# A two-layer decoder trunk on one core: VectorE takes over GpSimd's work at three entries, and the first loads are reordered

## The chip, the cores and the metric

One core of a Trainium2 chip runs the whole program. The metric is the device time of one execution in microseconds (us). The kernel before took 1767.41 us in the median of three runs (1766.88 to 1770.72). TensorE (PE) does the matrix products, ScalarE (ACT) and VectorE (DVE) the elementwise work, GpSimd (POOL) a little of it too; SyncE (SP) issues nearly all loads.

## The reference

256 tokens of 1024 channels go through two layers. A condition vector gives shift, scale and gate per channel (adaLN). Each layer has a mixer (convolution branch and chunkwise retention with rotary angles, one common input projection `w_in`) and a channel part: a dense SwiGLU in layer 0, eight experts with the top two per token in layer 1. After each part stands a post-norm residual.

```python
c_act = jax.nn.silu(c)
for l in range(DEPTH):
    ada = c_act @ w_ada[l] + b_ada[l]
    shift1, scale1, gate1, shift2, scale2, gate2 = ...
    h = x * (1.0 + scale1) + shift1
    mix = token_mixer(h, positions, w_in[l], ...)
    x = layer_norm(DEEPNORM_ALPHA * x + gate1 * mix, ln1_g[l], ln1_b[l])
    h = x * (1.0 + scale2) + shift2
    ff = swiglu(h, ...) if l % 2 == 0 else moe_swiglu(h, ...)
    x = layer_norm(DEEPNORM_ALPHA * x + gate2 * ff, ln2_g[l], ln2_b[l])
```

## The kernel before

**Precision and units.** Every product is done in three: a weight block `wf` (1 MB, 128x2048) is split into a high half `wh` (a cast on ACT, line 1678) and a low half `wl` (a subtraction on DVE, line 1680), 1024 columns at a time, and so are the activations (hH and hL, rH and rL, mH and mL, aH and aL, hgH and hgL). PE then adds wh·hi, wh·lo and wl·hi. A unit of the program is one such block with the function that uses it; `prog` is the list of units and of pieces of code between them, and the last loop of `_emit` walks it, splits some pieces ahead (`look`, `split_to`, at most six halves in buffers), runs what was deferred (`defer(k, f)`: k splits later), and issues a load as soon as a buffer was consumed. Each engine works through its own list in that order; only semaphores tie them.

**Start (lines 215 to 250, 658 to 712).** For k from 0 to 7 a column block `adat` (summed against the condition on DVE, line 260, into `adac`) is followed by an S block of `w_in`. `first_h` makes h of 128 channels on POOL: fh, hH, hL (lines 674 to 677). `products` then adds the block's 48 matmuls into eight banks (line 661). `rope_tables` makes the sine and cosine of the positions (lines 1069 to 1087). The loads on SP stand in the order: condition, columns, positions, column block 0, two blocks of xT, S block 0, the rest of xT.

**Entries of the dense layer and of layer 1's mixer.** `out_units` ends the part before: tile 0 (128 tokens) is normalized (`z_norm`), tile 1 after it. `boundary` gives what comes next: units of the gate (`fill`), `tile_to_h` for each tile (transposes, then hf_t with the new shift and scale, then hHn on ACT and hLn on POOL, line 388), and `close_ln`, which updates x with the norm's own g and b on POOL (lines 405 and 406, four steps of 128x1024), then closes the buffers. `T_unit` (dense) or `V_unit(0, ...)` (mixer) does the first products of tile 0 before tile 1 is ready. The buffers of the next stage (`sg`, `v`) lie where g and b lay.

**Entry of the experts (`moe`).** `ahead(4, pool)` has POOL split the first four low halves. Each tile is transposed (`turn`), routed (`logits`, `top`, `rank`, `onehot`), turned back (`back`) and split (`split_h`: hTH, hTL); x is updated on POOL; four `gather` steps make the experts' rows (hgH on ACT, hgL on DVE). The first two expert blocks are loaded into the buffers that hgH and hgL take later. `whole_h` adds hT on POOL. After that the experts' units follow, six matmuls of 512 columns for each split piece.

Of the kernel before, what the change touches and what calls it, by code (L numbers as in the profile page):

```python
# [12 lines left out]
F32 = mybir.dt.float32  # L13
# [4 lines left out]
ALU = mybir.AluOpType  # L18
PSUM = bass.MemoryType.PSUM

P = 128
# [23 lines left out]
OPEN = (11, 19, 27)  # L45
HFL = 999
XS = 10
AZL = 238
AHF = -0.5
VS = 0  # L50
# [10 lines left out]
CL = (5, 2)  # L61
CD = (2, 3)
BK = (4, 4)
EARLY = (2, 2, 0)
BEF = (0, -1)
LOOK = (4, 4)
COJ = 0
# [46 lines left out]
def _emit(tc, ctx, a):  # L114
# [47 lines left out]
    def code(fn):  # L162
        prog.append(fn)
# [49 lines left out]
    def setup():  # L213
        row, one = mixc["cst"][0:1, 0:D], sel[0:1, :]
        cb = state["cb"] = state["hp0"].tile([P, D], F32, name="cb", tag="on")
        sp.dma_start(row, a["c"])
        pool.memset(one, 1.0)
        for q in range(2):
            ps = tp_bank()
            mm(ps, one, row[:, q * 512:(q + 1) * 512], True, True)  # L220
            act.activation(cb[:, q * 512:(q + 1) * 512], ps, AF.Silu)
        sp.dma_start(cols, a["cols"])
        sp.dma_start(mixc["pi"], a["pos"].partition_broadcast(P))
        st["go"] = True
        issue_dma(1)
        sp.dma_start(mixc["xT"][:, 0:2, :], a["xT"][:, 0:2, :])
        issue_dma(2)
        sp.dma_start(mixc["xT"][:, 2:8, :], a["xT"][:, 2:8, :])

        make_identity(nc, ident)  # L230
        dve.tensor_copy(adab.rearrange("p l n -> p (l n)"), col("b_ada", 0, L * 48))
        for n in (1, 4):
            v = adab[:, :, n * 8:n * 8 + 8]
            dve.tensor_scalar(v, v, 1.0, None, op0=ALU.add)
# [92 lines left out]
    def hold(on):  # L327
        if not on:
            st["hold"] = None
        elif st["hold"] is None:  # L330
            st["hold"] = st["cur"]
# [72 lines left out]
    def x_update(z, t):  # L404
        pool.tensor_tensor(x[:, t, :], z[:, t, :], state["g"], op=ALU.mult)
        pool.tensor_tensor(x[:, t, :], x[:, t, :], state["b"], op=ALU.add)

    def load_gb(p, l, which):
        g = p.tile([P, D], F32, name="gbuf")
# [29 lines left out]
    def mixer(l, raws, bound, fill=(), tail=()):  # L439
# [139 lines left out]
        def V_unit(h, half):  # L579
            def fn(s, w, wl):  # L580
                k0 = half * 4 + s * 2
                if k0 == 0:
                    R["V"] = [mm_bank(), mm_bank()]
                    R["held"] = []
                ts_block(R["V"][0], w, wl, state["hH"], state["hL"], k0, 2, tsl(0), k0 == 0, k0 == 6)
                state.pop("second_tile", nothing)()
                if h == 0 and l:
                    hold(True)
                    R["held"].append((w, wl, k0))
                    if k0 < 6:  # L590
                        return
                    hold(False)
                else:
                    R["held"] = [(w, wl, k0)]
                for (w_, wl_, k_) in R["held"]:
                    ts_block(R["V"][1], w_, wl_, state["hH"], state["hL"], k_, 2, tsl(1), k_ == 0, k_ == 6)
                run_bg(BG[l])
                if k0 == 6:
                    if h == 0 and l and VS:
                        split_to(st["cur"] + VS)  # L600
                    v = R["hp"].tile([P, 2, 512], F32, name="v")
                    for t in range(2):
                        act.copy(v[:, t, :], R["V"][t])
                    R["v", h] = v
            return named(f'V{l}', Unit(W["v"][h, half], 2048, fn))
# [60 lines left out]
        def first_h(k):  # L666
            def fn():
                if k == 0:
                    state["hH"] = keep.tile([P, 8, T], F32R, name="hH0", tag="hH")
                    state["hL"] = keep.tile([P, 8, T], F32R, name="hL0", tag="hL")  # L670
                v = adac[:, 0, 0:16].rearrange("p (n k) -> p n k", n=2)[:, :, k]
                dve.tensor_tensor(v, v, adab[:, 0, 0:16].rearrange("p (n k) -> p n k", n=2)[:, :, k], op=ALU.add)
                f = R["hp"].tile([P, T], F32, name="fh", tag="rot0", bufs=2)
                pool.tensor_scalar(f, mixc["xT"][:, k, :], adac[:, 0, 8 + k:9 + k], adac[:, 0, k:k + 1],
                                   op0=ALU.mult, op1=ALU.add)
                pool.tensor_copy(state["hH"][:, k, :], f)
                pool.tensor_tensor(state["hL"][:, k, :], f, state["hH"][:, k, :], op=ALU.subtract)
                have["h", k] = True
                products(k)
            return fn  # L680

        if l == 0:
            code(open_pool)
            code(lambda: state.update(hp0=R["hp"]))
            code(setup)
            for what, k in START:
                if what == "a":
                    u = ada_cols(0, 0, k, first_h(k))
                    u.look = 0
                    if k == 0:  # L690
                        code(lambda: rope_tables(R["hp"]))
                else:
                    u = S_unit(k)
                prog.append(u)
            code(lambda: R.update(y=keep.tile([P, 8, T], F32, name="ycv", tag="z")))
            code(setup_late)
        else:
            first, t0, second, t1, close = bound
            prog.extend(first)
            code(t0)  # L700
            prog.extend(second)
            code(lambda: state.update(second_tile=t1))
            prog.append(V_unit(0, 0))
            prog[-1].look = 2
            if BEF[1] >= 0:
                prog[-1].before = (first + second)[BEF[1]]
            code(close)
            code(open_pool)
            prog.append(V_unit(0, 1))
            units += [A_unit(i) for i in range(6)]  # L710
        for h in range(H):
# [227 lines left out]
    def boundary(ada, nfx):  # L939
        fill = gate_fill(ada, ("lnp", "fx", nfx))  # L940

        def tile_to_h(t):
            z, (gcol, bcol) = state["z"], state["mc"]
            if t == 0:
                state["hH"] = keep.tile([P, 8, T], F32R, name="hHn", tag="hH")
                state["hL"] = keep.tile([P, 8, T], F32R, name="hLn", tag="hL")
            h_from(state["lnp"], z[:, t, :], t, gcol, bcol, "AA" if t == 0 else "DD", (pool, pool))

        return fill[0:2], (lambda: tile_to_h(0)), fill[2:4], (lambda: tile_to_h(1)), close_ln

    def close_ln(update=True):
        flush_deferred()
        for t in range(2 * update):
            x_update(state["z"], t)
        state.pop("lns").close()
        state.pop("lnp")
        if state.get("ffn") is not None:
            state.pop("ffn").close()
# [13 lines left out]
    def ffn(raws, bound):  # L972
# [10 lines left out]
        def T_unit(half):  # L983
            def fn(s, w, wl):
# [8 lines left out]
                if k0 < 6:  # L993
                    return
                hold(False)
                for (w_, wl_, k_) in R["held"]:
                    ts_block(R["b"][1], w_, wl_, state["hH"], state["hL"], k_, 2, tsl(1), k_ == 0, k_ == 6)
                for t in range(2):
# [37 lines left out]
        prog[-1].look = 2  # L1036
        if BEF[0] >= 0:
            prog[-1].before = (first + second)[BEF[0]]
        code(close)
        code(open_pool)  # L1040
        prog.append(T_unit(1))
        units = [GU_unit(j) for j in range(2, KF)]
        rest = [r[0] for r in raws[len(raws) - NREST:]]
# [45 lines left out]
    def moe():  # L1089
# [132 lines left out]
                                      op0=ALU.is_equal)  # L1222
            R["oh", pair] = oh

        def whole_h():
            R["hT"] = keep.tile([P, 2, D], F32, name="hT", tag="z")
            pool.tensor_tensor(R["hT"], R["hTH"], R["hTL"], op=ALU.add)
            state["keep"] = keep

        def chunk(kp):  # L1230
            h = R["hT"][:, :, 2 * kp * P:(2 * kp + 2) * P]
# [240 lines left out]
        def ahead(n, eng=dve):  # L1472
            code(lambda: split_to(pos_of[units[0].idx, 0] + n - 1, eng))

        for u in fill:
            u.look = 0
        ahead(4, pool)
        code(lambda: turn(0, "AA"))
        prog.extend(fill[0:2])
        code(lambda: logits(0))  # L1480
# [2 lines left out]
        code(lambda: turn(1, "AD"))  # L1483
        code(lambda: back(0))
        code(lambda: split_h(0))
        code(lambda: logits(1))
        code(lambda: back(1))
        code(lambda: state.update(hfx=R["p"]))
# [2 lines left out]
        prog.append(fill[3])  # L1491
        code(lambda: onehot(0))
        code(lambda: split_h(1))
        for t in range(2):
            code(lambda t=t: x_update(state["z"], t))
        code(lambda: defer(XS, lambda: act.activation(x, x, AF.Copy, scale=ALPHA)))
        for kp in range(4):
            if kp == 0:
                code(open_hg)
            o = slice(2 * kp * P, (2 * kp + 2) * P)  # L1500
            code(lambda kp=kp, o=o: gather(0, kp, (R["hTH"][:, :, o], R["hTL"][:, :, o]), mm_bank))
            if 1 <= kp <= 2:
                ahead(4 + kp)
        code(whole_h)
        prog.append(units[0])
        code(lambda: close_ln(False))
        code(open_acts)
# [144 lines left out]
    def issue_dma(upto=None):  # L1652
        while st["dma"] < (len(units) if upto is None else upto):
# [6 lines left out]
            mine.append(u.idx)  # L1660
            live.append(p)
            u.wf = p.tile([P, 2048], F32, name="wf", tag=tag, bufs=bufs)
            sp.dma_start(u.wf[:, 0:u.n], u.src)
            u.w = {}
            u.issued = True
            st["dma"] += 1
# [144 lines left out]
```

## Time and profile before

| | |
|---|---|
| median of 3 runs | 1767.41 us |
| profiled execution | 1769.15 us, span 1767.4 us |
| PE busy | 1700.4 us (96%) |
| DVE busy | 1556.2 us (88%) |
| ACT busy | 1157.4 us (65%) |
| POOL busy | 144.0 us (8%) |
| mean granted clock of PE | 0.987 of full |

The profile is one execution; its times start with the span. A row of the timeline gives start, duration, engine, line, operation and tiles, and in brackets how long the engine was idle before it and what ended the wait. Busy time is no proof of a limit: an engine's busy span may hold a wait inside an instruction. PE's clock has two levels here, 1.00 and 0.50 of full.

### The profile page before, as it was taken

The numbers are of one execution on the slowest core, as the hardware profiler recorded it, in microseconds if no ns is written. First come the engines' busy times: TensorE is split into PE (matmuls) and PEld (weight loads), VectorE is DVE, ScalarE is ACT, GpSimd is POOL, SyncE is SP. The second block draws the span as 40 slices with busy tenths as digits, with TensorE's granted clock in tenths as the row PEclk, the third lists the DMA queues.
The fourth block names the chain that finished last, engine by engine and source line by source line (L and its number), as shares of the span: only waits on it lengthen the run. The fifth ranks groups of instructions, "written<-read, shape, count | busy, mean of one in ns | idle before, by whom it ended". The sixth has DMA issues, their size and how long they took to land. (4 is left out here: it accounts for less than half of the span.)

```text
span 1767.4 us, 23998 instructions
## 1 busy us (share of the span) xinstructions
PE 1700.4 (96%) x8896; PEld 1431.5 (81%) x8896; DVE 1556.2 (88%) x2126; ACT 1157.4 (65%) x1625; POOL 144.0 (8%) x102
## 2 busy tenths in 40 slices
PE   6999999999999999999997999999999999999996
PEld 5978877669998698888886888888888888887885
DVE  7799989876778679999878999999999999998996
ACT  3566787643444365567543878778787878787783
POOL 5300000022000300000005000200002000100001
PEclk9999999999999999999997999999999999999998
DMA  9644457866789454445575889899998999898891
GB/s 363 257 167 145 165 205 288 310 258 243 281 305 352 176 191 167 167 170 188 188 281 238 325 324 378 328 357 378 362 372 312 398 350 383 314 373 329 333 342 63
DMA packets 71102, 491.60 MB, mean 278 GB/s; under 512 B 7953, under 2 KB 8721, under 8 KB 13634
## 3 DMA queue, kind: packets, MB, share of 16 engines
q1 hardware_dynamic: 69122, 484.28, 73.1%
q0 software_dynamic: 1568, 5.45, 0.9%
q8 instruction: 72, 1.18, 0.3%
q14 instruction: 52, 0.43, 0.1%
q10 hardware_dynamic: 288, 0.26, 0.0%
HBM read 488.92 MB, written 1.05 MB: 277 GB/s over the span
## 5 line engine op out<-in xcount | busy, mean ns | idle before, releaser
L1680 DVE TENSOR_TENSOR wl<-wf,wh 128x1024 fp32r<-128x1024 f32 x815 | 991.9, 1247 | 87.1 <-ACT wh L1678 74.1
L1678 ACT CAST wh<-wf 128x1024 fp32r<-128x1024 f32 x819 | 840.7, 1051 | 170.7 <-PE ps_mm L137 104.2
L137 PE MATMUL ps_mm<-wh,hgH 128*128 128x512 f32 x704 | 282.6, 401 | 0.0
L137 PE MATMUL ps_mm<-wh,hgL 128*128 128x512 f32 x704 | 275.1, 391 | 0.0
L137 PE MATMUL ps_mm<-wl,hgH 128*128 128x512 f32 x704 | 274.5, 390 | 0.0
L468 ACT ACTIVATE tap<-upad,cols 128x256 f32<-128x256 f32 x300 | 130.1, 505 | 74.9 <-DVE ycv L480 74.6
L137 PE MATMUL ps_mm<-hHn,wh 128*128 128x256 f32 x576 | 164.6, 286 | 0.5 <-ACT wh L1678 0.5
L137 PE MATMUL ps_mm<-hHn,wl 128*128 128x256 f32 x576 | 163.7, 284 | 0.8 <-DVE wl L1680 0.8
L137 PE MATMUL ps_mm<-hLn,wh 128*128 128x256 f32 x576 | 163.7, 284 | 0.0
L137 PEld LDWEIGHTS ps_mm<-wh,hgL 128*128 128x128 f32 x704 | 132.1, 188 | 27.9
L137 PEld LDWEIGHTS ps_mm<-wl,hgH 128*128 128x128 f32 x704 | 132.5, 188 | 26.0 <-issue 1.0
L137 PEld LDWEIGHTS ps_mm<-wh,hgH 128*128 128x128 f32 x704 | 132.2, 188 | 25.8 <-issue 1.0
L137 PE MATMUL ps_mm<-wh,mb 128*128 128x512 f32 (+1 forms) x476 | 145.8, 380 | 0.0
L137 PEld LDWEIGHTS ps_mm<-hHn,wh 128*128 128x128 f32 x576 | 111.2, 193 | 1.2 <-ACT wh L1678 0.7
L137 PEld LDWEIGHTS ps_mm<-hHn,wl 128*128 128x128 f32 x576 | 111.3, 193 | 1.0 <-DVE wl L1680 1.0
L137 PEld LDWEIGHTS ps_mm<-hLn,wh 128*128 128x128 f32 x576 | 111.3, 193 | 0.4 <-issue 0.2
L137 PEld LDWEIGHTS ps_mm<-wh,mb 128*128 128x128 f32 x476 | 87.9, 188 | 17.5 <-issue 1.5
L480 DVE TENSOR_TENSOR ycv<-ycv,tap 128x1024 f32<-128x1024 f32 (+1 forms) x90 | 94.0, 1045 | 5.6 <-ACT tap L468 4.2
L137 PE MATMUL ps_mm<-wl,mb 128*128 128x512 f32 (+1 forms) x238 | 89.8, 377 | 0.0
L137 PE MATMUL ps_mm<-wh,hHn 128*128 128x512 f32 x208 | 84.5, 406 | 0.0
L137 PE MATMUL ps_mm<-wh,hLn 128*128 128x512 f32 x208 | 81.3, 391 | 1.7 <-POOL hLn L388 1.7
L137 PE MATMUL ps_mm<-wl,hHn 128*128 128x512 f32 x208 | 81.2, 390 | 0.1
(307 smaller groups left out, 2947.2 us busy)
## 6 DMA issues: line engine op xcount, KB each, us to landing
wf<-moe_gu SPq DMA_DIRECT2D x176, 1024.0 KB, 7.0
wf<-moe_d SPq DMA_DIRECT2D x75, 1024.0 KB, 6.5
wf<-adat SPq DMA_DIRECT2D x32, 1024.0 KB, 6.1
wf<-ws SPq DMA_DIRECT2D x24, 1024.0 KB, 5.1
wf<-ffn_gu SPq DMA_DIRECT2D x20, 1024.0 KB, 6.4
wf<-v SPq DMA_DIRECT2D x16, 1024.0 KB, 4.9
wf<-g SPq DMA_DIRECT2D x16, 1024.0 KB, 4.9
wf<-f SPq DMA_DIRECT2D x16, 1024.0 KB, 4.9
```

Source lines behind the costliest of these rows:

```text
L137: pe.matmul(out, lhsT, rhs, start=start, stop=stop)
L468: act.activation(t[:, c - c0, :], u[:, c, j:j + T], AF.Copy, scale=taps[:, c, j:j + 1])
L480: dve.tensor_tensor(y, y, prod[j][:, 0:n, :], op=ALU.add)
L1678: act.copy(w[:, 0:m], src)
L1680: eng.tensor_tensor(wl[:, 0:m], src, w[:, 0:m], op=ALU.subtract)
```

## The change

- Start: the first two units are loaded in two halves each; the positions come after S block 0, column block 1 before the rest of xT. The angle tables are made ahead of the second column block instead of the first (`ROPE`). h of block 0 is made by DVE (fh, hL) and ACT (hH) instead of POOL; blocks 1 to 7 stay on POOL.
- Dense layer and layer 1's mixer: hLn moves from POOL to DVE for both tiles; half of tile 1's hf_t moves from DVE to ACT (`"AD"`); x is updated by DVE, in four steps that are deferred by `XD`. The old buffers are closed, and the new ones opened, inside the unit (`turned`) instead of after it.
- Experts: the first four low halves are split by DVE, one of them in front of the end of tile 1's sums (`EARLY[2]`), one after the first `split_h`, two after the second. x is updated and hT added by DVE, most of it deferred past the first expert unit.

```diff
+ROPE = 1
+XD = (1, 2, 3, 3)
-EARLY = (2, 2, 0)
+EARLY = (2, 2, 1)
...
         sp.dma_start(cols, a["cols"])
-        sp.dma_start(mixc["pi"], a["pos"].partition_broadcast(P))
         st["go"] = True
         issue_dma(1)
         sp.dma_start(mixc["xT"][:, 0:2, :], a["xT"][:, 0:2, :])
         issue_dma(2)
+        sp.dma_start(mixc["pi"], a["pos"].partition_broadcast(P))
+        issue_dma(3)
         sp.dma_start(mixc["xT"][:, 2:8, :], a["xT"][:, 2:8, :])
...
+    def x_steps(z):
+        def step(t, first):
+            if first:
+                dve.tensor_tensor(x[:, t, :], z[:, t, :], state["g"], op=ALU.mult)
+            else:
+                dve.tensor_tensor(x[:, t, :], x[:, t, :], state["b"], op=ALU.add)
+        return [lambda t=t, first=first: step(t, first) for t in range(2) for first in (True, False)]
...
                     hold(False)
+                    state.pop("turned", nothing)()
...
+                if k == 0:
+                    dve.tensor_scalar(f, mixc["xT"][:, k, :], adac[:, 0, 8 + k:9 + k], adac[:, 0, k:k + 1],
+                                      op0=ALU.mult, op1=ALU.add)
+                    act.copy(state["hH"][:, k, :], f)
+                    dve.tensor_tensor(state["hL"][:, k, :], f, state["hH"][:, k, :], op=ALU.subtract)
+                    have["h", k] = True
+                    products(k)
+                    return
...
-                    if k == 0:
+                    if k == ROPE:
                         code(lambda: rope_tables(R["hp"]))
...
-            code(close)
-            code(open_pool)
+            code(lambda: state.update(turned=lambda: (close(), open_pool())))
...
-            h_from(state["lnp"], z[:, t, :], t, gcol, bcol, "AA" if t == 0 else "DD", (pool, pool))
+            h_from(state["lnp"], z[:, t, :], t, gcol, bcol, "AA" if t == 0 else "AD", (dve, dve))
+            if t:
+                for n, f in enumerate(x_steps(z)):
+                    defer(XD[n], f)
...
-    def close_ln(update=True):
+    def close_ln(*_):
         flush_deferred()
-        for t in range(2 * update):
-            x_update(state["z"], t)
...
-            pool.tensor_tensor(R["hT"], R["hTH"], R["hTL"], op=ALU.add)
+            dve.tensor_tensor(R["hT"][:, t, :], R["hTH"][:, t, :], R["hTL"][:, t, :], op=ALU.add)
...
-        ahead(4, pool)
         code(lambda: turn(0, "AA"))
...
         code(lambda: split_h(0))
+        ahead(2)
         code(lambda: logits(1))
...
         code(lambda: split_h(1))
-        for t in range(2):
-            code(lambda t=t: x_update(state["z"], t))
-        code(lambda: defer(XS, lambda: act.activation(x, x, AF.Copy, scale=ALPHA)))
+        ahead(4)
+        steps = []
+        code(lambda: steps.extend(x_steps(state["z"])))
...
-            if 1 <= kp <= 2:
-                ahead(4 + kp)
-        code(whole_h)
+            if kp <= 1:
+                ahead(5 + kp)
+        code(lambda: [steps.pop(0)() for _ in range(2)])
+
+        def rest():
+            for n in range(2):
+                defer(1 + n, steps[n])
+            for n in range(2):
+                defer(2 + n, lambda n=n: whole_h(n))
+            defer(3, lambda: act.activation(x, x, AF.Copy, scale=ALPHA))
+        code(rest)
         prog.append(units[0])
...
-            sp.dma_start(u.wf[:, 0:u.n], u.src)
+            for o in range(0, u.n, 1024 if u.idx < 2 else u.n):
+                o = slice(o, min(u.n, o + 1024) if u.idx < 2 else u.n)
+                sp.dma_start(u.wf[:, o], u.src[:, o])
```

On SP the loads at the start stood in this order in the kernel before (`adat` the column blocks, `s` the S blocks, `cos` the buffer of the positions):

```order
L222 DMA cols<-cols 128x777
L223 DMA cos<-pos 128x256
L1663 DMA wf<-adat 128x2048
L226 DMA xT<-xT 128x512
L1663 DMA wf<-s 128x2048
L228 DMA xT<-xT 128x1536
L1663 DMA wf<-adat 128x2048
```

And in the changed kernel:

```order
L224 DMA cols<-cols 128x777
L1695 DMA wf<-adat 128x1024 x2
L227 DMA xT<-xT 128x512
L1695 DMA wf<-s 128x1024 x2
L229 DMA cos<-pos 128x256
L1695 DMA wf<-adat 128x2048
L231 DMA xT<-xT 128x1536
```

The positions went from the second place to behind S block 0, and the first two blocks come in halves.

On DVE at the entry of the dense layer, from the normalized tile 1 to the dense layer's aa, it was before:

```order
L402 TENSOR_SCALAR z<-z,ryf,nb 128x1024
L1680 TENSOR_TENSOR wl<-wf,wh 128x1024
L379 TENSOR_SCALAR hf_t<-ps_tp,gb 128x128 x8
L1680 TENSOR_TENSOR wl<-wf,wh 128x1024
L296 TENSOR_TENSOR gate<-ps_tp,gbias 128x512 x2
L1680 TENSOR_TENSOR wl<-wf,wh 128x1024 x2
L1003 TENSOR_TENSOR aa<-sg,ps_mm 128x256 x2
```

And now:

```order
L391 TENSOR_TENSOR hLn<-hf_t,hHn 128x4x128 x2
L1712 TENSOR_TENSOR wl<-wf,wh 128x1024
L382 TENSOR_SCALAR hf_t<-ps_tp,gb 128x128 x4
L391 TENSOR_TENSOR hLn<-hf_t,hHn 128x4x128 x2
L1712 TENSOR_TENSOR wl<-wf,wh 128x1024
L299 TENSOR_TENSOR gate<-ps_tp,gbias 128x512
L414 TENSOR_TENSOR x<-z,gbuf 128x1024
L1712 TENSOR_TENSOR wl<-wf,wh 128x1024 x2
L299 TENSOR_TENSOR gate<-ps_tp,gbias 128x512
L416 TENSOR_TENSOR x<-x,bbuf 128x1024
L414 TENSOR_TENSOR x<-z,gbuf 128x1024
L416 TENSOR_TENSOR x<-x,bbuf 128x1024
```

Four hLn and four x steps came in, and four of the eight hf_t went; the x steps stand behind the splits that the unit itself needs.

On DVE at the entry of the experts, from the second `split_h` on (gbuf and bbuf the norm's g and b), it was before:

```order
L1178 TENSOR_TENSOR hTL<-ps_sc,hTH 128x512 x2
L1243 CAST hgL<-ps_mm 128x512 x2
L1680 TENSOR_TENSOR wl<-wf,wh 128x1024
L1243 CAST hgL<-ps_mm 128x512
L1680 TENSOR_TENSOR wl<-wf,wh 128x1024
L1243 CAST hgL<-ps_mm 128x512
L296 TENSOR_TENSOR gate<-ps_tp,gbias 128x512
L1680 TENSOR_TENSOR wl<-wf,wh 128x1024
L296 TENSOR_TENSOR gate<-ps_tp,gbias 128x512
L1680 TENSOR_TENSOR wl<-wf,wh 128x1024 x2
```

And now:

```order
L1198 TENSOR_TENSOR hTL<-ps_sc,hTH 128x512 x2
L1712 TENSOR_TENSOR wl<-wf,wh 128x1024 x2
L1265 CAST hgL<-ps_mm 128x512
L1712 TENSOR_TENSOR wl<-wf,wh 128x1024
L1265 CAST hgL<-ps_mm 128x512
L1712 TENSOR_TENSOR wl<-wf,wh 128x1024
L1265 CAST hgL<-ps_mm 128x512 x2
L414 TENSOR_TENSOR x<-z,gbuf 128x1024
L416 TENSOR_TENSOR x<-x,bbuf 128x1024
L299 TENSOR_TENSOR gate<-ps_tp,gbias 128x512
L414 TENSOR_TENSOR x<-z,gbuf 128x1024
L1712 TENSOR_TENSOR wl<-wf,wh 128x1024
```

Behind the last row follow the last x step, two hT (128x1024 each) with the second gate step between them, and then the eighth split.

## Rows read from the trace of the kernel before

**Rows 1.** Table by stretches: stretch, its length, busy PE, PEld, DVE, ACT, POOL, clock, DMA.

```profile
409.70:413.00 3.30, 3.30 (x18) 3.30 (x17) 2.68 (x4) 1.11 (x3) 0.00 (x0) 0.50 1.07 298
946.00:969.00 23.00, 16.90 (x76) 14.83 (x77) 17.70 (x39) 6.49 (x13) 11.55 (x5) 0.50 0.33 128
1000.00:1200.00 200.00, 200.00 (x922) 165.44 (x921) 192.09 (x216) 158.86 (x198) 12.56 (x9) 1.00 0.93 352
```

**Rows 2.** DMA issues from 1.4 to 3.3 us: KB, then us to landing.

```profile
wf<-adat SPq DMA_DIRECT2D x1, 1024.0 KB, 7.8
```

**Rows 3.** Timeline of DVE, and one of ACT, at the start: start, duration, operation.

```profile
7.34 0.29 DVE L1069 CAST ang<-cos 128x256 f32<-128x256 int32 x1 [2.44 <-DMA cos<-pos]
...
11.34 0.29 DVE L1086 TENSOR_SCALAR nrot<-nrot 128x256 f32<-128x256 f32 x1
...
14.10 2.36 DVE L1680 TENSOR_TENSOR wl<-wf,wh 128x1024 fp32r<-128x1024 f32 x2
17.40 1.76 DVE L260 SCALAR_TENSOR_TENSOR wf<-wf,cb 128x1024 f32<-128x1024 f32 x1 [0.94 <-DMA wf<-adat]
...
13.02 1.99 ACT L1678 CAST wh<-wf 128x1024 fp32r<-128x1024 f32 x2 [0.93 <-DMA wf<-s]
```

**Rows 4.** Timeline of PE and POOL at the start.

```profile
17.32 0.58 PE L661 MATMUL ps_mm<-hH,wh 128*128 128x256 f32 x1 [11.09 <-POOL hH L676]
...
26.71 3.57 POOL L674 TENSOR_SCALAR fh<-xT,adac 128x256 f32<-128x256 f32 x1 [2.54 <-DVE adac L672]
...
49.94 1.59 POOL L677 TENSOR_TENSOR hL<-fh,hH 128x256 fp32r<-128x256 f32 x1
```

**Rows 5.** Timeline of DVE, PE and ACT at the dense layer's entry.

```profile
390.58 2.63 DVE L379 TENSOR_SCALAR hf_t<-ps_tp,gb 128x128 f32<-128x128 f32 x8
...
391.99 1.12 PE L137 MATMUL ps_tp<-asb,sel 128*128 128x512 f32 x2 [1.55 <-DVE hf_t L379]
...
407.73 0.66 ACT L1002 ACTIVATE sg<-ps_mm 128x256 f32<-128x256 f32 x2 [11.00 <-POOL x L406]
...
408.62 0.77 PE L1008 MATMUL ps_tp<-ident,aa 128*128 128x128 f32 x4 [2.20 <-DVE aa L1003]
```

**Rows 6.** Timeline of PE and ACT at the entry of layer 1's mixer.

```profile
598.27 1.13 PE L137 MATMUL ps_tp<-asb,sel 128*128 128x512 f32 x2 [1.55 <-DVE hf_t L379]
...
616.10 0.39 PE L137 MATMUL ps_mm<-hHn,wh 128*128 128x256 f32 x1 [0.53 <-ACT wh L1678]
...
617.36 0.39 PE L137 MATMUL ps_mm<-hHn,wl 128*128 128x256 f32 x1 [0.76 <-DVE wl L1680]
...
614.03 1.07 ACT L603 COPY v<-ps_mm 128x512 f32<-128x512 f32 x2 [11.03 <-POOL x L406]
```

**Rows 7.** Timeline of DVE, POOL and PE at the entry of the experts.

```profile
932.74 0.22 DVE L191 SCALAR_TENSOR_TENSOR rq<-ryf,hv 128x1 f32<-128x1 f32 x1
...
937.01 0.69 DVE L392 SCALAR_TENSOR_TENSOR z<-ps_mm,gate 128x512 f32<-128x512 f32 x1 [1.02 <-PE ps_mm L137]
937.74 2.77 DVE L393 SCALAR_TENSOR_TENSOR z<-x,z 128x512 f32<-128x512 f32 x1
...
947.57 2.19 DVE L191 SCALAR_TENSOR_TENSOR rq<-ryf,hv 128x1 f32<-128x1 f32 x1
...
951.58 1.88 DVE L1158 CAST ls<-idx 128x2 f32<-128x2 uint32 x1
953.49 2.54 DVE L1160 TENSOR_SCALAR E<-mcst,ls 128x8 f32<-128x8 f32 x2
...
979.30 4.98 DVE L1680 TENSOR_TENSOR wl<-wf,wh 128x1024 fp32r<-128x1024 f32 x4
...
947.39 2.34 POOL L406 TENSOR_TENSOR x<-x,bbuf 128x1024 f32<-128x1024 f32 x1
...
951.04 1.97 PE L367 MATMUL ps_sc<-ident,z 128*128 128x128 f32 x8 [8.47 <-DVE z L402]
...
970.87 0.79 PE L137 MATMUL ps_mm<-wh,hgH 128*128 128x512 f32 x1
```

More of the change, by code (lines that the diff above doesn't have):

```diff
@@ L995, in fn @@
                 hold(False)
+                state.pop("turned", nothing)()
                 for (w_, wl_, k_) in R["held"]:
@@ L1038, in ffn @@
             prog[-1].before = (first + second)[BEF[0]]
-        code(close)
-        code(open_pool)
+        code(lambda: state.update(turned=lambda: (close(), open_pool())))
         prog.append(T_unit(1))
@@ L1223, in onehot, with whole_h @@
             R["oh", pair] = oh
-        def whole_h():
-            R["hT"] = keep.tile([P, 2, D], F32, name="hT", tag="z")
-            pool.tensor_tensor(R["hT"], R["hTH"], R["hTL"], op=ALU.add)
-            state["keep"] = keep
+        def whole_h(t):
+            if t == 0:
+                R["hT"] = keep.tile([P, 2, D], F32, name="hT", tag="z")
+            dve.tensor_tensor(R["hT"][:, t, :], R["hTH"][:, t, :], R["hTL"][:, t, :], op=ALU.add)
+            if t:
+                state["keep"] = keep
         def chunk(kp):
```

## The prediction

> **What bounds the kernel now.** I read the page first: TensorE (PE) is busy 1700.4 of 1767.4 us, so a change can only win where PE stands still or runs at half clock. The table by stretches says where not to look: inside the experts, 1000 to 1200 us, PE is busy all 200 us at full clock, VectorE (DVE) 192 and GpSimd (POOL) 13 [rows 1]. So I listed PE's idle gaps over 0.25 us in the timeline and went through the four places that the diff touches, engine by engine. In the start, PE's first matmul waits 11.09 us for POOL's hH [rows 4]. At the entry of the dense layer PE stands 1.55 us behind DVE's hf_t and 2.20 us behind aa, which stands behind ACT's sg; that one waited 11.00 us for POOL's last update of x [rows 5]. The same pattern stands at the entry of layer 1's mixer: 1.55, 0.53 and 0.76 us, with ACT's v waiting 11.03 us for POOL [rows 6]. At the entry of the experts PE stands 8.47 us behind the normalization of tile 1 [rows 7], and from 946 to 969 us it runs at half clock [rows 1].
>
> The reason is told by one operation in two states. A 128x1 step of the reciprocal square root takes 0.22 us on DVE at 932.74; at 947.57 it takes 2.19 us, and POOL's x step runs from 947.39 for 2.34 us [rows 7]. DVE and POOL wait for each other whole instructions long. POOL suffers as much: its 128x256 fh takes 3.57 us at 26.71, beside DVE's splits [rows 4].
>
> **Start: +0.9 us.** Removed: POOL's three steps for block 0; the angle tables (7.34 to 11.63, 4.3 us) no longer stand before the first column sums [rows 3]. What is late next: the first column block lands 7.8 us after its issue [rows 2], so about 9.9; half of it, loaded as an own DMA and without the positions ahead of it, about 8.2 (half of the 2.5 us that one block takes in the full queue, and 0.3 for the positions). DVE sums 8.2 to 10.7, makes fh and hL with ACT's hH between, about 12.2. The S block landed at 13.0, where ACT's cast starts [rows 3]; its first half about 11.4. PE can start near 12.5 instead of 17.32 [rows 4].
>
> Then comes the price. DVE splits this S block (2.36 us [rows 3]) to about 15.2, and only now makes the tables, to 19.5. The second column block, which DVE took up at 17.40 as it landed [rows 3], is taken up at 19.5, without POOL beside it (2.4 us in place of 2.9): block 1's columns are done at 22.0 instead of 20.4, block 2's at about 27.2 instead of 26.5. From there the chain of before stands: POOL takes up block 2 at 26.71 and block after block until hL of block 5 ends at 51.53 (49.94 and 1.59) [rows 4], and PE has then three blocks of 48 matmuls over 256 columns, at least 5.2 us each (half of the 0.217 of a 512-column one in the experts, 922 in 200 us [rows 1]), to 67 or 68. So PE starts 4.8 us earlier, runs out of work in block 1 and ends the stage with the DVE chain: later by 0.7, taken as 0.9 because PE stands before block 1 and may lose clock there (a fall costs half of a stretch like that at 409.7, some 1.7 us [rows 1]). Ends: -2 (POOL's chain has slack and follows the earlier start), +3.5 (POOL's block 1 is shut out as block 2 was, for 3.57 us, and the whole chain moves by it).
>
> The split loads are where a rule speaks against the change. The row shows 7.8 us from issue to landing for 1 MB that queued behind others [rows 2]. The Trainium skill (DMA: Bandwidth & Descriptors, section on measured bandwidth) says to batch transfers to 1 MiB or more, each having a fixed cost of about 2 us; by that the second halves would land some 2 us later and the start would stand at +2.9. Blocks behind each other in one queue landed 2.5 us apart here, though each took over 7, so the fixed part overlaps. I leave it out of the sum; it lies inside the upper end.
>
> **Entry of the dense layer: -4.8 us.** hL of tile 0 moves to DVE behind z: done at 387.9 instead of 388.3, so the transposes of tile 1 are 0.5 earlier. Half of hf_t moves to ACT, which was idle: its four take about 1.4 us (DVE's eight take 2.63 [rows 5]; bounds 1.3 and 2.6), and the bank that the gate's matmul waits for is free at 391.0 instead of 391.94: PE's 1.55 us shrink to 0.5, -1.0. DVE then carries four x steps, 128x1024 with two inputs like a split, 1.25 us each (four in 4.98 us) [rows 7]: 5.0 us, in a stretch where DVE, too, ended up idle behind sg. With a split and two gate steps between them they end near 403.0 instead of 407.7, PE's next transposes stand ready at 405.5, sg and aa come at 403 to 404.3, so the gap of 2.20 goes, and with it the half clock of 409.7, 1.7 us [rows 1, 5]. Sum 1.0 + 2.1 + 1.7. If DVE were late by 1.2 us more, the gap would come back in part: ends -1.5 and -6.
>
> **Entry of layer 1's mixer: -2.5 us.** The same: 1.2 of the 1.55, and the 0.53 and 0.76 [rows 6]. Ends -0.5 and -3.5.
>
> **Entry of the experts: -7.7 us.** The normalization of tile 1: five DVE steps are stretched, the first from 0.69 (as its neighbour at 937.01) to 2.77 at 937.74, the last from 0.22 to 2.19 at 947.57 [rows 7], in sum 8.6 us. The split now put before it costs 1.25, of which 1.02 lies in DVE's wait for PE at 937.01 [rows 7]. So z ends at 942.6 instead of 950.99.
>
> From there to the first expert matmul it was 19.8 us (951.04 to 970.87 [rows 7]). Off go the stretches of two top-k steps, 1.88 and 2.54 beside POOL [rows 7], which undisturbed are like the 0.22 above and twice that: 3.9. Off go 2.7 for the clock: PE's 16.9 us between 946 and 969 [rows 1] would be 8.5 less at full clock, and I count a third, since PE will have pauses there too. On come the four splits that now stand between z and the second hgL, 1.25 each: 5.0. So 18.2 us, and a start near 960.8, 10.1 earlier. Of that DVE gives some back: PE wants the eighth split after seven of 1.3 us (six matmuls of 0.217) and 1.4 for the gate's matmuls, near 971.3. DVE, done with the second hgL at about 959.4, has three splits (3.75), two hgL and two gate steps (0.69 each), four x steps and two hT (1.25 each) to go: 14.0, so 973.4. Stall 2.1, and 0.3 more at the small steps of the expert weights: -7.7. Ends: -10.5 (no stall) and -2 (all 7.5 us of x and hT show).
>
> **Sum.** +0.9 - 4.8 - 2.5 - 7.7 = -14.1. The profiled execution took 1769.15 us (span 1767.4): 1755.0. The median of the runs, 1767.41, lies 1.7 lower: 1753.
>
> **Rivals.** First, DVE is the pace at the experts: for it speaks its 192 of 200 us [rows 1], against it that PE had no gap there. Then all 7.5 us and the split come back: entry -1.5 to -2, in all about 1759.
>
> Second, the clock. Before, PE's rare matmuls from 946 on left it at half rate until the gathers had run [rows 1]; in the changed kernel PE still has short work between DVE's steps from 944 to 960. If it stays at half rate into the experts' first splits, the 2.7 us for the clock are not won and the first splits cost 0.3 us of stall more: 3 us back, 1756. The Trainium skill (TensorE: Matmul & The Clock Gate, section on psum-queue depth-cycling) describes that many short idles between groups of matmuls make the clock fall and rise again; the half clock of 946 to 969 agrees, that shorter gaps do the same no row here shows.
>
> Third, the early start holds: POOL, with a block less to do, is not shut out of block 1, DVE's sums of blocks 1 and 2 run without it, and the stage ends 4 us earlier instead of 0.9 later: 1748.
>
> Fourth, slower: DVE as the pace at all three entries. It gets 6.2 us more at each of two (hL 2.5, x 5.0, less 1.3 of hf_t) and 12.5 at the experts (four splits, four x, two hT), 25 in all, and gets back the 8.6 us and, taken as as much again, all else that POOL stretches: +8, with the start 1776. It decides from the point where DVE has no idle time left before PE's next need. Against it: DVE stood idle behind sg and v.
>
> Last, the lock is not the cause: the steps stay long with POOL silent; then x and hT come on top and the entries' gains pay for them: 1767.
>
> **Chances.** Forecast 0.62, with its own range 1749 to 1757; first rival 0.13, second 0.10, third 0.07, fourth 0.04, last 0.04. Two hundredths of the first two I count as no change, for what I have overlooked. Range 1746 to 1762: it holds the first four cases, and leaves the slow one and no change out. Faster by over 0.2% (3.5 us, about what a measurement of this kernel can tell from no change) 0.90, within it 0.06, slower 0.04.
>
> **What would show it.** Start: first block matmul at 12 to 13 us, a wait of PE before block 1, and hL of block 5 about 1 us later than 51.53. Dense entry: sg without a POOL wait, no half clock near 405. Experts' entry: every 128x1 step of tile 1 at 0.16 to 0.22 us, the gap of 8.47 under 1 us, the first expert matmul near 961 and a first wait for wl, of some 2 us, at the eighth split. The forecast is wrong if the steps stay at 2 us without POOL, or if PE waits for wl again and again through the first expert.

## The result, and the profile after

The changed kernel takes 1755.93 us in the median of six runs (1753.84 to 1758.00), beside 1768.58 of the kernel before: ratio 0.9927, 95% interval 0.9914 to 0.9940. A second timing beside other runs gave 1754.58 us (1752.45 to 1756.82), ratio 0.9916 (0.9903 to 0.9929). The forecast's sum, 14.1 us less, was measured as 12.7 and 14.0 less.

| profiled execution | before | after |
|---|---|---|
| span | 1767.4 us | 1756.2 us |
| PE busy | 1700.4 | 1697.6 |
| DVE busy | 1556.2 | 1557.8 |
| ACT busy | 1157.4 | 1158.4 |
| POOL busy | 144.0 | 82.7 |
| granted clock | 0.987 | 0.989 |

PE has the same 8896 matmuls in the same order in all kernels told of here. So the start of any one of them can be subtracted between two traces; where that difference changes, time was won or lost. The table gives the change over each stretch (minus is won), named by the times of the kernel before:

| kernel (one profiled execution each) | start, to 80 | to 385, no edit | dense entry, to 500 | to 586, no edit | mixer entry, to 800 | experts, 925 to 1200 | at 1200 |
|---|---|---|---|---|---|---|---|
| after | +0.9 | +1.8 | -4.9 | -0.1 | -2.9 | -5.8 | -10.9 |
| after, again | +1.0 | +0.1 | -4.9 | -1.3 | -2.9 | -5.8 | -13.8 |
| start alone | +1.5 | +1.2 | -0.2 | -0.4 | 0.0 | -0.6 | +1.5 |
| the two entries alone | +0.3 | +0.4 | -4.9 | +0.9 | -2.9 | -0.5 | -6.8 |
| experts' entry alone | 0.0 | -0.2 | 0.0 | -1.7 | 0.0 | -8.2 | -10.1 |

Where no edit stands, the executions of this table differ by up to 2.6 us (-1.7 to +0.9 in the stretch to 586). The two entries repeat to 0.1 us; the experts' term does not (-5.8 and -8.2). The rows behind them, in the order of the groups ahead of the prediction. First the table by stretches (stretch, its length, busy PE, PEld, DVE, ACT, POOL, clock, DMA), to be read beside [rows 1]:

```profile
28.09:69.77 41.68, 41.68 (x336) 41.68 (x337) 31.78 (x42) 13.00 (x17) 31.17 (x18) 0.96 0.88 342
406.00:409.40 3.40, 3.40 (x31) 3.40 (x30) 2.94 (x5) 2.61 (x5) 0.00 (x0) 1.00 0.41 154
942.60:952.90 10.30, 8.03 (x33) 5.87 (x34) 7.42 (x21) 6.18 (x9) 0.00 (x0) 0.50 0.57 214
976.70:980.10 3.40, 3.40 (x10) 2.73 (x11) 3.40 (x5) 3.40 (x5) 0.00 (x0) 0.51 1.02 417
1000.00:1200.00 200.00, 200.00 (x920) 165.14 (x919) 191.86 (x215) 158.61 (x197) 12.18 (x9) 1.00 0.92 352
```

Inside the experts nothing changed. At the dense entry the half clock is gone. Ahead of the experts 10 us at half clock are left of 23, and a new piece stands at 976.7. The start, on PE and POOL, answers to [rows 4]:

```profile
12.27 0.58 PE L673 MATMUL ps_mm<-hH,wh 128*128 128x256 f32 x1 [6.25 <-ACT wh L1710]
...
26.36 0.58 PE L673 MATMUL ps_mm<-hH,wh 128*128 128x256 f32 x1 [5.27 <-POOL hH L696]
...
28.09 0.58 PE L673 MATMUL ps_mm<-hL,wh 128*128 128x256 f32 x1 [1.15 <-POOL hL L697]
...
21.41 3.57 POOL L694 TENSOR_SCALAR fh<-xT,adac 128x256 f32<-128x256 f32 x1 [19.72 <-DVE adac L684]
...
50.10 1.59 POOL L697 TENSOR_TENSOR hL<-fh,hH 128x256 fp32r<-128x256 f32 x1
```

PE starts 5 us earlier, does block 0, and stands 5.27 and 1.15 us before block 1, whose fh took POOL 3.57 us. From 28.09 on it never waits in this stage (first row of the table by stretches). The two entries, PE and ACT, answer to [rows 5, 6]:

```profile
390.55 0.51 PE L139 MATMUL ps_mm<-wh,hLn 128*128 128x512 f32 x1 [0.50 <-DVE hLn L391]
...
393.79 0.70 PE L139 MATMUL ps_tp<-asb,sel 128*128 128x512 f32 x1 [1.16 <-ACT hf_t L380]
...
408.06 0.60 PE L1029 MATMUL ps_tp<-ident,aa 128*128 128x128 f32 x4
...
594.98 0.70 PE L139 MATMUL ps_tp<-asb,sel 128*128 128x512 f32 x1 [1.16 <-ACT hf_t L380]
...
392.23 1.51 ACT L380 ACTIVATE hf_t<-ps_tp,gb 128x128 f32<-128x128 f32 x4 [1.01 <-PE ps_tp L370]
...
405.41 0.66 ACT L1023 ACTIVATE sg<-ps_mm 128x256 f32<-128x256 f32 x2 [7.65 <-PE ps_mm L139]
...
606.60 1.07 ACT L615 COPY v<-ps_mm 128x512 f32<-128x512 f32 x2 [7.64 <-PE ps_mm L139]
```

sg and v wait for PE now, no longer for POOL, and PE does not wait for aa. The first row, PE's wait for hL of tile 0, stood in the kernel before as:

```profile
388.37 0.50 PE L137 MATMUL ps_mm<-wh,hLn 128*128 128x512 f32 x1 [1.03 <-POOL hLn L388]
```

The experts' entry, on DVE, ACT and PE, answers to [rows 7]:

```profile
932.64 0.69 DVE L396 SCALAR_TENSOR_TENSOR z<-x,z 128x512 f32<-128x512 f32 x1
...
935.80 0.22 DVE L193 SCALAR_TENSOR_TENSOR rq<-ryf,hv 128x1 f32<-128x1 f32 x1
...
936.44 0.81 DVE L405 TENSOR_SCALAR z<-z,ryf,nb 128x1024 f32<-128x1024 f32 x1
...
970.79 1.28 ACT L1219 ACT_TABLE_LOAD   x1
973.13 0.20 ACT L1219 ACTIVATE e<-d 128x2 f32<-128x2 f32 x1 [1.06 <-DVE d L1218]
973.35 1.28 ACT L1298 ACT_TABLE_LOAD   x1
...
954.61 0.79 PE L139 MATMUL ps_mm<-wh,hgH 128*128 128x512 f32 x1
...
967.07 0.50 PE L139 MATMUL ps_mm<-wl,hgH 128*128 128x512 f32 x1 [0.74 <-DVE wl L1712]
...
976.57 0.55 PE L1304 MATMUL ps_tp<-ident,maa 128*128 128x128 f32 x2 [1.85 <-ACT pt L1275]
```

Tile 1's steps have their short length, PE's wait of 8.47 us is gone, and the first expert matmul comes 16.3 us earlier than in [rows 7], of which 5.1 had been won upstream. Then PE waits 0.74 us for wl, at the eighth split, and 1.85 us for pt (the transposed placement of an expert's rows), which ACT writes behind two table loads and a wait for DVE's d.

### The profile page after: what moved, and what is told of

The parts are those of the page before. It is cut to its first block, busy times and chain, and to the rows that moved or that the text cites. A ratio compares the mean times of both kernels' runs of the same rounds, so it can differ in the third digit from the quotient of the medians.

```text
span 1756.2 us, 23986 instructions
## 1 busy us (share of the span) xinstructions
PE 1697.6 (97%) x8896; PEld 1427.3 (81%) x8896; DVE 1557.8 (89%) x2146; ACT 1158.4 (66%) x1634; POOL 82.7 (5%) x74
```

## Experiments

**The parts alone.** start_only, entries_only and experts_only each apply one of the three parts of the diff to the kernel before.

> The start's part alone (loads, angle tables ahead of the second column block, h of block 0 on VectorE and ScalarE). In the trace of the changed kernel PE stood 0.9 us later than before at the end of this stage, and 1.7 us more were lost near the end of layer 0's mixer, where nothing was edited. Theory A, the later loss belongs to the start (PE arrives in another phase to the same loads): +2.7 us, ratio about 1.0015, and the trace shows PE 2.7 us later at the entry of the dense layer. Theory B, the later loss was an accident of that execution: +0.9 us, ratio 1.0005. Theory C, the early start pays: -4 us, ratio 0.998.

Measured: 1769.79 us beside 1769.10, ratio 1.0003 (0.9994 to 1.0012). Theory C is out, and A's 1.0015 lies outside. This one trace does look like A: PE is 2.6 us late at the dense entry, 1.2 of it lost in the stretch up to 385. But the kernels told of here that have the same start lose between -1.0 (exp_early) and +1.8 us in that stretch, so the later loss belongs to single executions. The start is worth nothing that can be told from zero.

> The part of the dense layer's entry and of layer 1's mixer alone (hL and x on VectorE, half of hf_t on ScalarE). My theory: the terms hold by themselves, -4.9 and -2.8 us as PE's lead in the changed kernel's trace, in all -7.7 us, ratio 0.9956; PE stands as before up to the entry of the dense layer. Rival: they owe part to the start (the other phase of the loads), then at most -5 us, ratio 0.997.

Measured: 1760.35 us, ratio 0.9944 (0.9931 to 0.9957). The 0.9956 of my theory is inside, the rival's 0.997 is not, and the trace shows the same -4.9 and -2.9 as with the other edits.

> The experts' entry alone (four low halves, x and hT on VectorE). My theory: -5.8 us, ratio 0.9967, made of -11 at the first expert matmul and 5.4 given back in the 35 us behind it, mostly where PE waits for ScalarE's pt behind the softmax of the two chosen experts. Rival: what is given back comes from the other edits (buffers and loads that arrive in another phase), then -10 us, ratio 0.994, and no wait for pt.

Measured: 1760.97 us, ratio 0.9956 (0.9941 to 0.9971); the trace won 8.2 us. The size lies between the two theories, but the wait for pt is there, 1.87 us, so what is given back comes from this edit:

```profile
978.98 0.33 PE L1294 MATMUL ps_tp<-ident,maa 128*128 128x128 f32 x1 [1.87 <-ACT pt L1265]
```

Of the 2.4 us that differ from the changed kernel's -5.8, 0.8 stand already at the first expert matmul (12.0 us won there in place of 11.2); most of the rest is the clock. By the table by stretches, the 3.4 us right behind this wait, here and in the changed kernel's second execution:

```profile
979.20:982.60 3.40, 3.40 (x17) 2.82 (x16) 3.40 (x5) 3.40 (x5) 0.00 (x0) 1.00 1.00 414
```

```profile
974.80:978.20 3.40, 3.40 (x10) 2.66 (x9) 3.40 (x4) 3.40 (x6) 0.00 (x0) 0.50 0.99 400
```

17 matmuls at full clock against 10 at half, some 1.6 us.

The changed kernel once more beside the runs told of further below:

> The changed kernel once more, beside the next three. The three parts alone gave +0.7, -8.8 and -8.1 us against the kernel before, in sum -16.2; the changed kernel's first timing gave -12.7. If the parts add and only the timings scatter: 1753 to 1756 (ratio 0.991 to 0.993). If the parts get into each other's way (one pace that gives back what another won): 1757 or more (0.9935).

Measured: 1754.58 us, ratio 0.9916 (0.9903 to 0.9929): the parts add, within what the timings tell.

**What the lock costs.** The lock is what the prediction takes the long steps for: VectorE and GpSimd hold each other up for whole instructions. pool_beside adds products that nobody needs to the changed kernel:

```diff
+        def beside():
+            src = state["z"][:, 0, :].rearrange("p (k n) -> p k n", k=8)
+            for _ in range(3):
+                pool.tensor_tensor(R["hf"][:, :, tsl(1)], src, src, op=ALU.mult)
+        code(beside)
         code(lambda: turn(0, "AA"))
```

> The changed kernel with three products of 128x1024 on GpSimd during the normalization of tile 1 at the experts' entry; they write a part of hf that is overwritten before it is read, so nobody needs them. Theory that VectorE and GpSimd wait for each other: VectorE's small steps beside them take some 2.2 us in place of 0.16 to 0.22, z of tile 1 ends 3 to 5 us later, and the kernel takes +4 us against the changed kernel (ratio to the kernel before about 0.995). Theory that the length of these steps came from what VectorE itself had to wait for, or from the order of the work: no step changes, 0.9927 as the changed kernel.

Measured: 1760.39 us, ratio 0.9946 (0.9933 to 0.9959), by the ratios 3.4 and 5.3 us above the changed kernel's two timings. POOL's three products run from 928.68 for 7.02 us. DVE's groups of operations in this stretch (operations of one shape, count, busy us, mean ns), here and in the changed kernel from 928 to 937:

```profile
L396 DVE SCALAR_TENSOR_TENSOR z<-x,z 128x512 f32<-128x512 f32 x2 | 3.8, 1910 | 0.1
L1717 DVE TENSOR_TENSOR wl<-wf,wh 128x1024 fp32r<-128x1024 f32 x1 | 2.2, 2189 | 0.0
L397 DVE BATCH_NORM_STATS2 zst<-z 128x6 f32<-128x512 f32 x2 | 1.4, 696 | 0.1
L395 DVE SCALAR_TENSOR_TENSOR z<-ps_mm,gate 128x512 f32<-128x512 f32 x2 | 1.4, 681 | 0.0
```

```profile
L397 DVE BATCH_NORM_STATS2 zst<-z 128x6 f32<-128x512 f32 x2 | 1.4, 694 | 0.1
L396 DVE SCALAR_TENSOR_TENSOR z<-x,z 128x512 f32<-128x512 f32 x2 | 1.4, 692 | 0.1
L395 DVE SCALAR_TENSOR_TENSOR z<-ps_mm,gate 128x512 f32<-128x512 f32 x2 | 1.4, 685 | 0.0
L1712 DVE TENSOR_TENSOR wl<-wf,wh 128x1024 fp32r<-128x1024 f32 x1 | 1.2, 1209 | 0.0
```

Nobody needs POOL's results and yet z<-x,z goes from 692 to 1910 ns and the split from 1209 to 2189: for these two the lock is shown. It is choosy: z<-ps_mm,gate, one of whose inputs lies in PSUM, and the statistics, with one input, keep their length. The Trainium skill (SBUF — State Buffer, section Who interferes with whom) says that a DVE instruction with two SBUF inputs contends with a GpSimd instruction that reads SBUF, that one in a two-port mode contends with GpSimd and the two block each other for the whole instruction, and that one with at most one SBUF input outside these modes does not contend. The trace agrees: 1910 against 692 ns with two SBUF inputs, 681 against 685 with one.

POOL was done before the 128x1 steps began, so these stayed at 0.16 to 0.22 us: what the forecast of this run said of them is not tested by it. That they are long beside POOL and short without it is seen only by comparing kernels with and without the experts' edit. For another small step experts_x_pool (below) has the test. Its cast of two columns, beside POOL's x, is long again, where the changed kernel has 0.17 us:

```profile
940.30 1.87 DVE L1178 CAST ls<-idx 128x2 f32<-128x2 uint32 x1
...
939.79 2.35 POOL L414 TENSOR_TENSOR x<-z,gbuf 128x1024 f32<-128x1024 f32 x1 [6.41 <-DVE ls L1175]
```

**POOL at the same places again.** In entries_x_pool and experts_x_pool the function `x_steps` gets the engine as an argument:

```diff
-                for n, f in enumerate(x_steps(z)):
+                for n, f in enumerate(x_steps(z, pool)):
```

> The changed kernel with the four x steps of the dense layer's entry and of layer 1's mixer on GpSimd again, issued at the same places; hL, hf_t and the later closing of the buffers stay as changed. Theory A, what the entries won is that sg and v no longer wait for GpSimd's last x: both waits come back (sg 11 us, then 2.2 of PE and a stretch at half clock), +5 us against the changed kernel, ratio 0.9945. Theory B, the gain is the order of the work and half of hf_t on ScalarE: +0 to 1 us.

Measured: 1765.56 us, ratio 0.9988 (0.9980 to 0.9997): by the ratios 11 to 13 us above the changed kernel, more than twice theory A, and not by its mechanism; sg did not wait for POOL. DVE, PE and POOL at the dense entry:

```profile
391.06 3.46 DVE L391 TENSOR_TENSOR hLn<-hf_t,hHn 128x512 fp32r<-128x512 f32 x2
394.44 3.37 DVE L1712 TENSOR_TENSOR wl<-wf,wh 128x1024 fp32r<-128x1024 f32 x1
...
391.79 0.79 PE L139 MATMUL ps_mm<-wh,hLn 128*128 128x512 f32 x1 [3.95 <-DVE hLn L391]
...
391.22 2.74 POOL L414 TENSOR_TENSOR x<-z,gbuf 128x1024 f32<-128x1024 f32 x1 [7.55 <-DVE z L405]
394.04 2.68 POOL L416 TENSOR_TENSOR x<-x,bbuf 128x1024 f32<-128x1024 f32 x1
```

"The same place" was an error of mine: POOL has nothing else to do, so x runs as soon as z is there, right beside hLn. The two instructions of hLn take 3.46 us (1.29 in the changed kernel), PE stands 3.95 us, and its mean clock from 391 to 395 is 0.57. At the mixer's entry the same happens: hLn takes 3.46 us again, PE stands 3.33 us, and the clock is 0.60 from 595 to 600 and 0.50 from 600 to 605. By the starts of the matmuls the dense entry stands at +0.8 in place of -4.9, the mixer's at +4.1 in place of -2.9.

> The changed kernel with x and hT at the experts' entry on GpSimd again, at the same places behind the gathers; the four low halves stay on VectorE. Theory A, VectorE is the pace there and 7.4 us of its work are what makes it late: PE's waits of 0.75 (wl) and 1.85 us (pt) go, -2 to -3.5 us against the changed kernel. Theory B, GpSimd's products stretch VectorE's splits beside them by more than they take off it: 2.2 us and more in place of 1.22, PE waits for wl, +1 to +4 us.

Measured: 1762.55 us, ratio 0.9964 (0.9951 to 0.9976), by the ratios 6.5 to 8.5 us slower than the changed kernel, again because x starts at once. Tile 0's two steps run on POOL from 928.20 for 5.2 us, beside z<-x,z (2.67 us in place of 0.69) and a split (2.67), and PE waits 3.28 us for z; tile 1's stretch the top-k steps, and hT two more splits (4.54 us for both). The trace splits the loss: at the first expert matmul PE is 12.7 us behind the second execution of the changed kernel (1.9 of it from upstream), at 1200 only 7.9. The waits for wl and pt do not occur. So theory A is wrong in the sum and right in its mechanism: with those 7.4 us off DVE, 0.3 us are given back behind the first expert matmul in place of 5.1. That PE comes late is not the reason: in pool_beside it comes 5.5 us late, DVE keeps the work, and 5.0 are given back. Theory B's stretched splits are there too, ahead of the first expert matmul.

**exp_early: where the softmax stands.** The difference d and its exponential move from `weights` into a function called in front of the x steps:

```diff
+        code(exps)
         code(lambda: [steps.pop(0)() for _ in range(2)])
```

> The changed kernel with the difference and the exponential of the softmax over the two chosen experts put right behind the last gather, where ScalarE stands idle 2.3 us, in place of six splits later. Theory A, the wait of 1.85 us for pt and the half clock behind it come from ScalarE standing 3.8 us in this spot (two table loads of 1.28 us and 1.06 us for VectorE's d): both go, -3.5 us against the changed kernel, ratio 0.9907. Theory B, VectorE is the pace there and ScalarE only passes it on: the wait turns up at the next wl, -0.5 to 0 us, 0.9927.

Measured: 1753.27 us, ratio 0.9911 (0.9899 to 0.9924), beside 0.9916 of the changed kernel in the same runs: no difference that can be told, and the interval leaves room for either theory. The wait for pt and the half clock behind it are gone, but PE now waits there for DVE itself:

```profile
974.11 0.30 PE L1308 MATMUL ps_tp<-ident,maa 128*128 128x128 f32 x1 [1.16 <-DVE maa L1303]
```

In kind that is theory B: the wait turns up at DVE. In size this one trace lies between: the experts' term is -8.1 us in place of -5.8, 1.6 of it the clock.

**The start without POOL.** start_dve has h of all blocks made by DVE and ACT; start_rope moves the tables behind the stage as well; start_cast is start_dve with one cast and one split per block put earlier:

```diff
# start_dve, for every k
+                    act.activation(state["hH"][:, k, :], mixc["xT"][:, k, :], AF.Identity,
+                                   bias=adac[:, 0, k:k + 1], scale=adac[:, 0, 8 + k:9 + k])
                     dve.tensor_scalar(f, mixc["xT"][:, k, :], ...)
# start_rope
-                    if k == ROPE:
-                        code(lambda: rope_tables(R["hp"]))
...
+            code(lambda: defer(2, lambda: rope_tables(R["hp"])))
# start_cast: ahead of the column sums, and between fh and hL
+                st["cast"](units[2 * k + 1], 0)
...
+                        st["split_to"](2 * k + 1, 0)
```

> The changed kernel with h of all eight blocks on VectorE (fh, hL) and ScalarE (hH, beside fh); the angle tables stay ahead of the second column block. In the changed kernel PE waits 5.3 us before block 1 for GpSimd's hH and then 1.1 for its hL, and runs 3 us of work at half clock. Theory A, GpSimd's block 1 is what held PE: VectorE's chain of some 5.95 us a block from 18.8 us on ends at 60, PE's stage at 63 to 64.5 in place of 69.8: -5.5 us against the changed kernel, ratio 0.9895. Theory B, the chain of VectorE is the bound and takes over what GpSimd gives up (1 us more a block): no gain, 0 to +1 us, 0.9927.

Measured: 1749.72 us, ratio 0.9897 (0.9881 to 0.9913): 4.9 us below the changed kernel of the same runs. In the trace the stage ends 2.2 us earlier than in the second execution of the changed kernel, not 5.5: the wait before block 1 is 2.23 us in place of 5.27, and then DVE is the pace at 6.45 us a block, two of whose waits show in its timeline:

```profile
27.52 0.43 DVE L691 TENSOR_TENSOR hL<-fh,hH 128x256 fp32r<-128x256 f32 x1 [0.22 <-ACT hH L687]
28.46 2.36 DVE L1713 TENSOR_TENSOR wl<-wf,wh 128x1024 fp32r<-128x1024 f32 x2 [0.51 <-ACT wh L1711]
```

Theory A for block 1, theory B for the rest. So the ratio meets theory A's 0.9895 in part by luck: a further 2.6 us of the trace's gain stand at the experts' entry (-8.4 in place of -5.8), where nothing was edited and the clock behind the wait for pt stayed full.

> As start_dve, and the angle tables, too, leave the stage: they are made behind it, two splits into the next units, just ahead of the first rotation. Theory A: VectorE's chain ends at 58 (the loads hold block 1), PE's stage at 61: -8.7 us against the changed kernel, ratio 0.988, less up to 2 us where the tables now stand. Theory B: the loads (a pair of blocks each 5 us) or the place of the tables take it back: no better than start_dve.

Measured: 1753.12 us, ratio 0.9911 (0.9897 to 0.9925): theory B. The stage ended earlier still, but the tables, 4.3 us of DVE at 77.78, met DVE without slack there, and up to 385 the trace gives back 2.8 us (a further 2.8, up to 586, lie where no edit stands):

```profile
86.36 0.50 PE L139 MATMUL ps_mm<-wl,hH 128*128 128x512 f32 x1 [2.36 <-DVE wl L1712]
```

> As start_dve, with the first cast of each S block put ahead of the column sums on ScalarE, and the first low half ahead of hL on VectorE. In start_dve VectorE's pace is 6.45 us a block, of which it waits 0.51 for wh and 0.22 for hH. Theory A, these waits are the bound: 5.75 us a block, PE's own pace; PE's stage ends at 61.5 to 62 in place of 67.6: -5 us against start_dve (1749.7), ratio 0.987. Theory B, the loads or ScalarE are next: -1 to -2 us.

Measured: 1745.19 us, ratio 0.9870 (0.9853 to 0.9887), theory A. From 22.49 us on PE never waits in the stage, at full clock, and ends it at 62.77, 7 us earlier than in the changed kernel:

```profile
22.49:62.77 40.28, 40.28 (x336) 40.28 (x336) 36.82 (x61) 18.24 (x25) 0.00 (x0) 1.00 0.97 366
```

> start_cast and exp_early together: if the two places are independent, their gains add: -1.3 us against start_cast, 1743 to 1748, the fastest of all.

Measured: 1744.34 us, ratio 0.9863 (0.9848 to 0.9878). It can't be told from start_cast, as exp_early couldn't from the changed kernel. In its profiled execution, the slowest of four, the start won 3.5 us where start_cast's won 6.1; DVE waited 0.91 us there for the second half of the first column block. Both beat the changed kernel, by the ratios by 8 to 11 us.

## Why the prediction was right, and where it was not

The total was right, and the terms held place by place (forecast, then the traces): start +0.9, +0.5 to +1.8 in seven executions with this start (without it the two of this table show 0.0 and +0.3); dense entry -4.8, -4.9 each time; mixer entry -2.5, -2.9; experts -7.7, -5.8 to -8.2. By times, the parts alone gave +0.7, -8.8 and -8.1. Their sum, -16.2, is more than the 12.7 to 14.0 measured together; each interval is about 2 us to either side, so that the parts hinder each other is not shown.

**Start: right number by luck, wrong chain.** PE did start near 12.5 (12.27) and did run dry before block 1. But block 1 was the case I had kept for the upper end: fh shut out for 3.57 us. And hL of block 5 ended 0.2 us later than in [rows 4], not 1: the chain made up the delay because POOL's fh of blocks 3 and 4 took 2.59 us each, where they had taken 3.64 and 3.65 before. What ended the stage was PE itself: 336 matmuls of the last seven blocks without a gap in 41.68 us, 5.95 a block with the half clock at its head, where my step put 5.2 (start_cast, at full clock throughout, needed 5.75). With that price PE could not have caught up with the chain. The trace of the kernel before could have told me: three blocks of 5.2 from 51.53 end at 67.1, and its stage ended at 68.9, about three blocks of 5.75. The rival in which the early start holds failed because POOL still made block 1; start_cast shows that it holds once POOL is out and DVE's waits are gone.

The halves did not cost the 2 us that would have put the start at +2.9. In the changed kernel ACT's casts of the two halves of S block 0 ran without a gap, 2.07 us for both; in other executions with the same loads DVE waited up to 0.91 us (best) for the second half of the column block. The Trainium skill (DMA: Bandwidth & Descriptors, section on measured bandwidth) says to batch transfers to 1 MiB or more. The waits that show here are 0.91 us at most. The fixed cost of about 2 us that I named with the rule stands in another section of that page of the Trainium skill, on the anatomy of one DMA, as a fit to loads that GpSimd issues; those here are issued by SP.

**Dense and mixer entries.** The term for hf_t was mis-sized: 1.55 us went to 1.16 at both entries, a gain of 0.4 in place of 1.0 and 1.2, since ACT's four steps did take 1.51 us, but start only behind PE's first transposes, and PE, through with these early, waits for the last of them. hL on DVE, which the sums had not counted, gave the rest: PE's wait for it went from 1.03 to 0.50, and at the mixer a wait of 0.62 went. That the totals agree is so far luck; the large terms of the dense entry, aa and the clock behind it, held. entries_x_pool adds what I had not priced: that the steps of x had to leave POOL and not only be issued elsewhere.

**Experts' entry.** z was forecast 8.4 us earlier: the PE row that waits for it came 8.5 earlier, upstream gains taken off. The first expert matmul was forecast 10.1 earlier; it came 11.2. The step that failed is what DVE gives back: one stall of 2.1 us at the eighth split, and 0.3 at the small steps. The stall was 0.74, and the small steps cost 1.85 us plus, in some executions, half clock behind it, in sum 5.4 of the 11.2 (3.8 of 12.0 in experts_only). That the term still came near -7.7 owes something to luck: more was won ahead of the first expert matmul, and more given back behind it. The first rival (DVE as the pace) was right for these 20 us and wrong for the rest; experts_x_pool and exp_early both point to DVE. The second rival came in part: the clock was at half from 942.6 for 10.3 us while PE had short work between waits, and full again by the first expert matmul. The Trainium skill (TensorE: Matmul & The Clock Gate, section on psum-queue depth-cycling) describes a clock that falls and rises again when PE is often idle for moments between groups of matmuls. The trace agrees in kind: in those 10.3 us PE was busy for 8.03, with waits of 1.86 and 0.68 us.

## What to carry to other kernels

When VectorE's tiny steps take 2 us in a trace, look at what GpSimd is doing in that moment: work that was handed to it because it stood idle lengthens the steps beside it that take two inputs from SBUF, and some others. An idle engine starts as soon as its inputs are there, so work can't be put later on it by moving the call. And price a new start by the pace of each engine behind it: an early first matmul is worth something only when the next block's inputs come at the engine's own pace.

## What I had not expected of the hardware

The same wait of 1.84 to 1.89 us before the transposes of maa was followed by 3.4 us at half clock in some executions and not in others of nearly the same work: half after the changed kernel's two, pool_beside's, entries_x_pool's and start_cast's, full after experts_only's, start_dve's and start_rope's. It decides some 1.6 us of the experts' term, and no row here says what tips it. And where no edit stands, PE's place moved by up to 4.5 us between executions (in the stretch to 586 from -1.7 in experts_only to +2.8 in start_rope), through waits for splits and half clock behind them; a term of that size is read from several executions or not at all.
